# The low halves of every second weight block formed by GpSimd in place of VectorE, in a hybrid pooling and SSD decoder layer

## The chip, the cores and the metric

The kernel runs on one core of a Trainium2 chip. A core has TensorE for matrix products (PE in the profile; its weight loads are PEld), VectorE (DVE), ScalarE (ACT), GpSimd (POOL) and SyncE (SP), and queues through which SyncE, ScalarE and GpSimd issue DMA transfers. The engines run at the same time, each through its own list of instructions in a fixed order, and wait for one another by semaphores. The metric is device microseconds of one execution, lower being better.

## The reference

One decoder layer over 512 tokens and 16 leading meta tokens, width 1024, all in float32. Cut to what matters:

```python
h = concat([meta, x]); u = rmsnorm(h, mix_norm_w)
proj = u @ w_in[i]                     # 1024 x 9248: pooling input, z, xBC, dt, two gates
gates = sigmoid(gate columns + b_gate)
y_pool = pool_mixer(u_pool, ...) @ w_pool_up      # causal means over 2, 4, 8, 16 positions
y_ssd = mamba2_branch(z, xbc, dt, ...) @ w_ssd_out  # conv, SSD in chunks of 128, 8 groups
h = h + (gate_pool * y_pool + gate_ssd * y_ssd) @ w_o
v = rmsnorm(h, mlp_norm_w)
hid = relu(v @ w_ff1); h = h + (hid * hid) @ w_ff2
return rmsnorm(h, final_norm_w)[:, 16:]
```

## The kernel before

Activations are kept transposed, features on the 128 partitions and tokens along the free axis. Every float32 operand of a product is split into two float32r tiles: a high half, the cast of the operand, and a low half, the operand less its high half. A product is then three matmuls: high by high, high by low, low by high.

**Weight blocks.** The weights come as 128x1024 blocks in the order in which they are used. `block_tiles` (line 63) takes the next number from the counter `nblk` and three tiles: `raw` from a ring of 3, `whi` and `wlo` from rings of 4. `block_part` (line 70) then issues three instructions: SyncE's load of `raw` (line 72), ScalarE's cast to `whi` (line 73) and VectorE's subtraction to `wlo` (line 74). The tiles of a block can be written again when the block that had them before is through on TensorE, so up to three blocks are prepared ahead. The same counter is advanced by loads of weights that don't pass through `block_part` (`wo_load`, line 706, and `quarter`, line 904); those are split by `split` (line 713, ScalarE's cast and VectorE's subtraction in lines 717 and 718).

**Stages in time.**
- Until about 68 us: the input norm, the first group's projections on the not yet normalised input, three gates, `dt` and its sums (lines 175 to 326 and 520 to 526).
- The loop over eight groups (line 562), about 68 to 484 us. For each group `ssd` (line 383) is woven with `group_proj` (line 351) of the next group. `ssd` loads `abc` by GpSimd's DMA queue (line 391) and makes decay factors of it on ScalarE and VectorE; VectorE multiplies them by the masked product of C and B (line 457, 128x2048), and TensorE takes the result as an operand of `py` (line 470). A chain of chunk states `st` runs beside it, on VectorE, two steps for each chunk (lines 455 and 456): the first reads two tiles in SBUF, the second one in SBUF and one in PSUM. TensorE takes the states as operands of `po` (line 464). `group_proj` takes up four projections `px` and, by `conv` (line 328), has ScalarE and VectorE read them out of PSUM (lines 331 and 334), then two projections `pz`. With group 4, `out_half` (line 544) forms half of the SSD output projection; with the last, `out_part` (line 552) a further part, which VectorE adds onto `acc` (line 559).
- About 484 to 563 us: the pooling branch (`pool_tile`, line 580, with running sums `pw` on VectorE in lines 593 and 595; `pool_mix`, line 603) and the last part of the SSD output projection, `psl`, added onto `acc` (line 633).
- About 563 to 640 us: the SSD gates and the pooling branch's projection, merged (lines 729 to 744); then the output projection by a Strassen-like scheme of seven products (lines 748 to 864), to about 690 us.
- The MLP (from line 867). There GpSimd forms sums of weight quarters (`sum_of`, line 965, its instruction in line 967).

Which instruction stands where on an engine is decided by a scheduler when the kernel is built, by its own estimates of durations; it keeps the data dependences and puts in the semaphores. An engine then runs its list in that order, so an instruction that waits holds all behind it on its engine. Beside its set-up, GpSimd has this list before: the four stores of `acs_d` (line 302), the eight loads `abc` (line 391), four loads of `ht` and one of `fw` (lines 754 and 755), and the 28 sums of line 967.

Of the kernel before, what the change touches and what calls it, by code (L numbers as in the profile page):

```python
# [9 lines left out]
F32 = mybir.dt.float32  # L10
F32R = mybir.dt.float32r
AF = mybir.ActivationFunctionType
ALU = mybir.AluOpType
# [36 lines left out]
def kernel(ctx: ExitStack, tc, xT, x, w, vec, fnw, out):  # L50
    nc = tc.nc
    act, dve, pe, pool = nc.scalar, nc.vector, nc.tensor, nc.gpsimd
# [6 lines left out]


    nblk = [0]

    def block_tiles():
        b = nblk[0]
        nblk[0] += 1
        return (b, wp.tile([P, 1024], F32, tag="raw", name=f"raw{b}", bufs=3),
                wp.tile([P, 1024], F32R, tag="whi", name=f"whi{b}"),
                wp.tile([P, 1024], F32R, tag="wlo", name=f"wlo{b}"))

    def block_part(t, c):  # L70
        b, raw, hi, lo = t
        nc.sync.dma_start(raw[:, c], w[b, :, c])
        act.copy(hi[:, c], raw[:, c])  # L73
        dve.tensor_tensor(lo[:, c], raw[:, c], hi[:, c].bitcast(F32), op=ALU.subtract)  # L74

    def block():
        t = block_tiles()
        block_part(t, slice(0, 1024))
        return t[2:]
# [8 lines left out]
    def mm3(ps, a, b, first, last):  # L88
        (ah, al), (bh, bl) = a, b
        pe.matmul(ps, ah, bh, start=first, stop=False)  # L90
        pe.matmul(ps, ah, bl, start=False, stop=False)  # L91
        pe.matmul(ps, al, bh, start=False, stop=last)  # L92
# [88 lines left out]
    b, raw, hi, lo = wdt  # L181
# [18 lines left out]
    dve.tensor_tensor(spread(lo)[:, :2], once[:, :2], spread(hi)[:, :2].bitcast(F32), op=ALU.subtract)  # L200
    x_split(0)
    block_part(wB, slice(0, 256))
    x_load(1)
    proj_step(dt_runs, 0, wdt[2:], X)
# [3 lines left out]
    dve.tensor_tensor(spread(lo)[:, 2:], once[:, 2:], spread(hi)[:, 2:].bitcast(F32), op=ALU.subtract)  # L208
    x_load(2)
    block_part(wB, slice(256, 1024))  # L210
    proj_step(dt_runs, 1, wdt[2:], X)
    proj_step(runsB, 1, wB[2:], X)
# [45 lines left out]
    for i in range(2):  # L258
        pb = psum1(f"pb1_{i}")
        c = slice(3 * i, 3 * i + 3)  # L260
# [77 lines left out]
    def group_tiles(g):  # L338
        xc = gc.tile([P, 2, L], F32, tag="xc", name=f"xc{g}")
        bt = gc.tile([P, L], F32, tag="bt", name=f"bt{g}")  # L340
        ct = gc.tile([P, SEQ], F32, tag="ct", name=f"ct{g}")
        zt = gc.tile([P, 2, SEQ], F32, tag="zt", name=f"zt{g}", bufs=1)
        return xc, bt, ct, zt
# [7 lines left out]
    def group_proj(g, cur, gate=None):  # L351

        first = g == 0
        xc, bt, ct, zt = cur
        for dst, t, skip in ((bt, 16 + g, 0), (ct, 24 + g, NM - 4), (xc[:, 0, :], 2 * g, 0),
                             (xc[:, 1, :], 2 * g + 1, 0)):
            if first and dst is bt:
                view = viewB
            else:
                runs, view = wide(psum2(f"px{g}_{t}"), skip)  # L360
                proj(runs, block(), X if first else U)
            conv(dst, first_raw(t, view, skip) if first else view, t)
            yield
        if gate is not None:
            gate_pool(gate)
            yield
        ps = psum2(f"pz{g}")
        for i in range(2):
            proj(narrow(ps[:, i * SEQ : (i + 1) * SEQ]), block(), X if first else U)
        zf = zt.rearrange("p i t -> p (i t)")  # L370
        if first:
            dve.tensor_tensor(zt, ps.rearrange("p (i t) -> p i t", i=2),
                              rsb[:, NM:].unsqueeze(1).to_broadcast([P, 2, SEQ]), op=ALU.mult)
            act.activation(zf, zf, AF.Silu)
        else:
            act.activation(zf, ps, AF.Silu)
        yield
# [125 lines left out]
    def weave(a, b, n):  # L503

        end = object()
        a = [a]
        while a or b:
            for s in [a] + [b] * n:
                if s and next(s[0], end) is end:
                    s.pop(0)  # L510
# [33 lines left out]
    def out_half():  # L544
        for dd in range(4):
            ps = psum2(f"pso{dd}")
            for i in range(2):
                ssd_out(2 * dd + i, ps[:, i * SEQ : (i + 1) * SEQ], range(8))
                act.copy(acc[2 * dd + i], ps[:, i * SEQ : (i + 1) * SEQ])
                yield  # L550

    def out_part():

        un = units()
        for d in range(NK):
            ps = psum2(f"psp{d}")[:, :SEQ]
            for k in range(8, 14):
                mm3(ps, next(un), ys[k], k == 8, k == 13)
            dve.tensor_tensor(acc[d], acc[d], ps, op=ALU.add)
            yield  # L560

    for g in range(G):
        nxt = group_tiles(g + 1) if g + 1 < G else None
        fill = [group_proj(g + 1, nxt, GATE_AT.get(g))] if nxt else [out_part()]
        if g == 4:
            fill = [out_half()] + fill
        weave(ssd(g, cur), fill, 2 if g == 4 else 1)
        cur = nxt
# [160 lines left out]
    for n, d in enumerate(MERGE):  # L729
# [8 lines left out]
        for i, k in enumerate(ks):  # L738
            c = slice(k * P, (k + 1) * P)
# [131 lines left out]
    def ff1_part(p, ks, first, last):  # L871
        ps, wh, wl = p
        for k in ks:
            cs = slice(k * P, (k + 1) * P)
            mm3(ps, (wh[:, cs], wl[:, cs]), (vh[k], vl[k]), first and k == ks[0], last and k == ks[-1])
# [7 lines left out]
    ff1_part(pf[1], range(4, 8), True, False)  # L883
    for p in pf:
        ff1_part(p, range(4), False, True)
    wo2_stack.close()
    mg_stack.close()
    wo_stack.close()
# [145 lines left out]
    c = NC - 1  # L1034
# [172 lines left out]
```

## Time and profile before

| what | value |
|---|---|
| time, median of 2 runs (lowest, highest) | 1025.61 us (1025.49, 1025.72) |
| span of the profiled execution, first to last instruction | 1023.3 us |
| time of the profiled execution beside its span | not given; the median is 2.3 us above the span |
| TensorE busy | 1014.6 us (99%) |
| VectorE busy | 730.3 us (71%), 954 instructions |
| ScalarE busy | 552.5 us (54%) |
| GpSimd busy | 88.7 us (9%), 52 instructions |
| granted TensorE clock, mean | 0.999 |
| DMA | 105.63 MB, 103 GB/s over the span |

Times in the profile are microseconds from the span's start, unless marked ns. A row of the timeline gives start, duration, engine, line, operation, the tiles written and read with their shapes and, in brackets, how long the engine had been idle before it and what ended that. Equal instructions that follow each other are one row, with their count. A group row gives busy time in us and mean duration in ns, then idle time before the instructions and who ended it. A row of the waits says which engine and line waited for which, for how many us in total, how many times, and the longest. A row of stretches gives the stretch and its length, busy time (and instructions) of PE, PEld, DVE, ACT and POOL, the granted clock, the DMA share and GB/s. Matmuls are pipelined and their ends are modelled, so their durations overlap.

### The profile page before, as it was taken

The page shows a single profiled execution, that of the slowest core. Times are in us where ns is not written, and L with a number is a line of the kernel's source. Part 1 is how long each engine was busy: PE and PEld are TensorE (multiplying, and loading weights), DVE is VectorE, ACT ScalarE, POOL GpSimd, SP SyncE. Part 2 cuts the span into 40 slices and gives each one's busy share as a digit, 9 for nine tenths or more (in the row PEclk, how much of TensorE's full clock was granted, in tenths as well). Part 3 has the DMA queues.
Part 4 walks back from the last instruction along what each step waited for, and adds up shares of the span by engine and source line. Part 5 has one row for each costly group of instructions (what it writes and reads, how often), then busy time and mean ns, then how long its engine had stood idle before and what let it go on. Part 6 is the DMA issues. An engine that isn't in the chain of part 4 may idle for free.

```text
span 1023.3 us, 14063 instructions
## 1 busy us (share of the span) xinstructions
PE 1014.6 (99%) x5697; PEld 876.7 (86%) x5697; DVE 730.3 (71%) x954; ACT 552.5 (54%) x728; POOL 88.7 (9%) x52
## 2 busy tenths in 40 slices
PE   9999999999999999999999999999999999999997
PEld 8889989998879898988899888888888888888886
DVE  7978788687746586978755457975777577666866
ACT  7775968586627339573244343474545355454444
POOL 0100000000000000000000001003040421413400
PEclk9999999999999999999999999999999999999999
DMA  7243051414332331414532333224323323334112
GB/s 237 72 160 103 21 166 38 148 46 141 102 101 86 103 104 42 145 41 141 189 102 84 103 104 120 86 91 156 103 69 122 120 83 113 95 102 124 42 42 83
DMA packets 29281, 105.63 MB, mean 103 GB/s; under 512 B 3296, under 2 KB 4256, under 8 KB 28192
## 3 DMA queue, kind: packets, MB, share of 16 engines
q1 hardware_dynamic: 26496, 92.75, 28.7%
q0 software_dynamic: 2000, 11.08, 3.0%
q8 instruction: 45, 0.74, 0.3%
q10 hardware_dynamic: 720, 0.91, 0.3%
q14 instruction: 20, 0.16, 0.1%
HBM read 102.55 MB, written 2.16 MB: 102 GB/s over the span
## 4 chain that ended last, share of the span: by engine, by line
PE 96%; DVE 2%; ACT 0%; DMA 0%; issue 0%; SPq 0%; ACTq 0%
PE px L143 6%; PE px L144 6%; PE pf L92 6%; PE pf L91 6%; PE px L146 6%; PE pf L90 6%; PE alpha L956 3%; PE alpha L957 3%; PE alpha L958 3%; PE pz L143 3%; PE pz L146 3%; PE pz L144 3%; PE py L470 2%; PE pso L90 2%; PE pp L144 2%; PE pp L146 2%
## 5 line engine op out<-in xcount | busy, mean ns | idle before, releaser
L73 ACT CAST whi<-raw 128x1024 fp32r<-128x1024 f32 (+1 forms) x131 | 135.7, 1043 | 220.0 <-PE pf L91 55.8
L74 DVE TENSOR_TENSOR wlo<-raw,whi 128x1024 fp32r<-128x1024 f32 (+1 forms) x131 | 163.6, 1251 | 112.6 <-ACT whi L73 105.3
L143 PE MATMUL px<-uh,whi 128*128 128x264 f32 (+1 forms) x448 | 121.2, 290 | 0.7 <-DVE ct L334 0.7
L144 PE MATMUL px<-ul,whi 128*128 128x264 f32 (+1 forms) x448 | 118.9, 285 | 0.0
L90 PE MATMUL pf<-vh,whi 128*128 128x512 f32 x256 | 99.8, 390 | 0.0
L92 PE MATMUL pf<-vh,wlo 128*128 128x512 f32 x256 | 99.6, 389 | 0.0
L91 PE MATMUL pf<-vl,whi 128*128 128x512 f32 x256 | 99.6, 389 | 0.0
L146 PE MATMUL px<-uh,wlo 128*128 128x264 f32 (+1 forms) x448 | 90.8, 284 | 0.0
L143 PEld LDWEIGHTS px<-uh,whi 128*128 128x128 f32 x448 | 84.6, 189 | 2.8 <-issue 2.6
L144 PEld LDWEIGHTS px<-ul,whi 128*128 128x128 f32 x448 | 84.8, 189 | 0.3
L718 DVE TENSOR_TENSOR slo<-b,shi 128x1024 fp32r<-128x1024 f32 x35 | 49.1, 1403 | 31.6 <-ACT shi L717 31.6
L146 PEld LDWEIGHTS px<-uh,wlo 128*128 128x128 f32 x448 | 69.4, 188 | 0.3 <-issue 0.3
L717 ACT CAST shi<-b 128x1024 fp32r<-128x1024 f32 x35 | 36.8, 1050 | 47.2 <-PE pf L91 36.4
L91 PEld LDWEIGHTS pf<-vl,whi 128*128 128x128 f32 x256 | 48.1, 188 | 10.0
L90 PEld LDWEIGHTS pf<-vh,whi 128*128 128x128 f32 x256 | 48.1, 188 | 9.9
L92 PEld LDWEIGHTS pf<-vh,wlo 128*128 128x128 f32 x256 | 48.1, 188 | 9.9
L967 POOL TENSOR_TENSOR b<-b,b 128x1024 f32<-128x1024 f32 x14 | 35.7, 2548 | 238.3 <-DVE slo L718 238.3
L956 PE MATMUL alpha<-shi,hh 128*128 128x512 f32 x140 | 54.6, 390 | 0.0
L957 PE MATMUL alpha<-slo,hh 128*128 128x512 f32 x140 | 54.5, 389 | 0.0
L958 PE MATMUL alpha<-shi,hl 128*128 128x512 f32 x140 | 54.5, 389 | 0.0
L783 DVE TENSOR_TENSOR ht<-ht,alpha 128x1024 f32<-128x1024 f32 x35 | 42.5, 1214 | 10.9 <-PE alpha L958 10.9
L143 PE MATMUL pz<-uh,whi 128*128 128x512 f32 x112 | 44.0, 393 | 0.0
(412 smaller groups left out, 2513.7 us busy)
## 6 DMA issues: line engine op xcount, KB each, us to landing
raw<-in_w SPq DMA_DIRECT2D x129, 512.0 KB, 3.6
b<-in_w SPq DMA_DIRECT2D x28, 512.0 KB, 3.6
abc<-acs_d POOLq DMA_DIRECT2D x8, 1024.0 KB, 7.2
wob<-in_w SPq DMA_DIRECT2D x8, 512.0 KB, 4.6
xt<-in_xT SPq DMA_DIRECT2D x8, 264.0 KB, 5.6
ht<-in_x POOLq DMA_DIRECT2D x4, 512.0 KB, 6.7
w<-in_w SPq DMA_DIRECT2D x4, 512.0 KB, 3.6
out_dram<-out SPq DMA_DIRECT2D x4, 320.0 KB, 2.4
```

The lines of the kernel that those rows point to most:

```text
L73: act.copy(hi[:, c], raw[:, c])
L74: dve.tensor_tensor(lo[:, c], raw[:, c], hi[:, c].bitcast(F32), op=ALU.subtract)
L90: pe.matmul(ps, ah, bh, start=first, stop=False)
L91: pe.matmul(ps, ah, bl, start=False, stop=False)
L92: pe.matmul(ps, al, bh, start=False, stop=last)
L143: pe.matmul(o, wh, rhs[0][k][:, c], start=k == 0, stop=False)
L144: pe.matmul(o, wh, rhs[1][k][:, c], start=False, stop=False)
L146: pe.matmul(o, wl, rhs[0][k][:, c], start=False, stop=k == NK - 1)
L718: dve.tensor_tensor(lo, src, hi.bitcast(F32), op=ALU.subtract)
L956: pe.matmul(ps[t], a[0], wh[:, cs], start=f, stop=False, skip_group_check=True)
L957: pe.matmul(ps[t], a[0], wl[:, cs], start=False, stop=False, skip_group_check=True)
L958: pe.matmul(ps[t], a[1], wh[:, cs], start=False, stop=l, skip_group_check=True)
```

## The change

From the loop over the groups on, a flag is set, and while it is set `block_part` gives the subtraction of a block with an odd number to GpSimd and that of an even one to VectorE. The flag is taken back after the first two blocks of the MLP's first product have been prepared; from there on all are VectorE's again. Operands, shapes and the numbers computed stay the same. By the counter this concerns 45 blocks. The scheduler, which sees the other engine, also places some instructions of TensorE, VectorE, ScalarE and SyncE otherwise, mostly within the loop over the groups.

```diff
@@ -59,6 +59,7 @@
     nblk = [0]
+    by_pool = [False]
 
     def block_tiles():
         b = nblk[0]
@@ -71,7 +72,8 @@
         b, raw, hi, lo = t
         nc.sync.dma_start(raw[:, c], w[b, :, c])
         act.copy(hi[:, c], raw[:, c])
-        dve.tensor_tensor(lo[:, c], raw[:, c], hi[:, c].bitcast(F32), op=ALU.subtract)
+        on = pool if by_pool[0] and b % 2 else dve
+        on.tensor_tensor(lo[:, c], raw[:, c], hi[:, c].bitcast(F32), op=ALU.subtract)
@@ -559,6 +561,7 @@
+    by_pool[0] = True
     for g in range(G):
         nxt = group_tiles(g + 1) if g + 1 < G else None
@@ -883,6 +886,7 @@
     for p in pf:
         ff1_part(p, range(4), False, True)
+    by_pool[0] = False
     wo2_stack.close()
```

## The prediction

> **What bounds the kernel now.** I read the busy shares first, then the chain that ended last, then the list of what TensorE waited for, then the engines' busy time stage by stage.
>
> ```profile
> PE 1014.6 (99%) x5697; PEld 876.7 (86%) x5697; DVE 730.3 (71%) x954; ACT 552.5 (54%) x728; POOL 88.7 (9%) x52
> PE 96%; DVE 2%; ACT 0%; DMA 0%; issue 0%; SPq 0%; ACTq 0%
> ...
> PE pdt L187 <- DVE ones_r L100: 1.5, 1, 1.5
> PE px L143 <- DVE ct L334: 0.7, 1, 0.7
> PE pdt L143 <- ACT xh L194: 0.2, 1, 0.2
> PE pt_dt L305 <- DVE ddt L294: 0.2, 1, 0.2
> ...
> 68.00:264.00 196.00, 195.32 (x1370) 177.56 (x1369) 152.47 (x242) 141.29 (x189) 2.12 (x4) 1.00 0.29 90
> 442.00:484.00 42.00, 42.00 (x225) 34.66 (x223) 38.46 (x54) 21.86 (x31) 0.00 (x0) 1.00 0.29 88
> 484.00:563.00 79.00, 79.00 (x526) 72.59 (x526) 50.56 (x66) 29.99 (x40) 0.00 (x0) 1.00 0.39 127
> 563.00:640.00 77.00, 77.00 (x338) 63.14 (x337) 45.81 (x64) 26.23 (x34) 2.60 (x5) 1.00 0.36 110
> ```
>
> TensorE is busy 99% of the span and is 96% of the chain. All its waits of the whole run are those four rows, 2.6 us, and three of them lie before the stretch that the change touches (about 57 to 680 us). Columns of the stretches are length, then PE, PEld, DVE, ACT, POOL. From 68 to 264 us TensorE lacks 0.68 us (196.00 less 195.32), the one wait of line 143 for VectorE's `ct`; in the three later stretches it lacks nothing. So whatever VectorE is spared, **at most 0.7 us can be won**. What can be lost is open: VectorE is busy 78% (152.47 of 196) and 92% (38.46 of 42) of the first two stretches, so it does not run far ahead of TensorE there.
>
> **What is removed and added.** The block counter runs over all weight blocks, so the odd ones from 11 to 85, then 89, 91, 95, 97, 101, 103 and 107 go over: 45 subtractions. (The counter is also advanced by the blocks that bypass this path, so near the end two of three neighbours can be odd.) DMAs, casts and matmuls stay, as does their number.
>
> ```profile
> L74 DVE TENSOR_TENSOR wlo<-raw,whi 128x1024 fp32r<-128x1024 f32 x86 | 104.8, 1220 | 74.2 <-ACT whi L73 66.9 <-PE po L464 7.3
> ...
> 755.68 1.22 DVE L783 TENSOR_TENSOR ht<-ht,alpha 128x1024 f32<-128x1024 f32 x1 [0.64 <-PE alpha L958]
> 756.82 1.79 DVE L74 TENSOR_TENSOR wlo<-raw,whi 128x1024 fp32r<-128x1024 f32 x1
> 761.98 2.33 DVE L718 TENSOR_TENSOR slo<-t,shi 128x1024 fp32r<-128x1024 f32 x1 [3.37 <-ACT shi L717]
> 764.24 1.21 DVE L74 TENSOR_TENSOR wlo<-raw,whi 128x1024 fp32r<-128x1024 f32 x1
> ...
> 755.12 2.41 POOL L967 TENSOR_TENSOR b<-b,b 128x1024 f32<-128x1024 f32 x1 [33.09 <-DVE slo L718]
> 757.61 3.25 POOL L967 TENSOR_TENSOR t<-b,b 128x1024 f32<-128x1024 f32 x1
> 760.82 2.40 POOL L967 TENSOR_TENSOR b<-b,b 128x1024 f32<-128x1024 f32 x1
> 764.39 3.32 POOL L967 TENSOR_TENSOR t<-t,b 128x1024 f32<-128x1024 f32 x1 [1.16 <-DVE slo L718]
> ...
> 712.05 2.89 DVE L938 TENSOR_TENSOR s<-r 128x512 f32<-128x512 f32 x1
> ```
>
> VectorE loses 45 x 1.220 = 54.9 us. GpSimd gains 45 operations of the shape that its sums of line 967 have: 2.40 us when nothing is beside them, up to 3.32, so 45 x 2.40 = 108 to 45 x 3.32 = 149 us in a stretch of 620. It is far from full.
>
> **The hold between the two engines.** These rows, all of the last stage, also show what the pairing costs. VectorE's `ht<-ht,alpha` (one operand in PSUM) ran in the middle of GpSimd's 755.12 operation in its usual 1.22. `wlo` and `slo`, with both operands in SBUF, did not: `slo` came at 761.98, GpSimd's operation ended at 763.22, and `slo` took 2.33 for 1.22, that is 763.2 plus its own length. Turned round, `wlo` began at 764.24 and the GpSimd operation of 764.39 took 3.32 for 2.40. So whoever comes second stands still until the first has ended. The dearest hold here is `s<-r` at 712.05, a 128x512 form that takes 0.68 elsewhere (the `acc` row below has that size): 2.89, a hold of 2.2. One moved block thus spares VectorE 1.22 and costs it between 0 and 2.2. The saving and the hold are about equal in sum; they are not equal in place. VectorE's queue had the subtraction *behind* the urgent work, GpSimd does it as soon as the cast is ready.
>
> The Trainium skill ("SBUF — State Buffer", Who interferes with whom) says that a VectorE instruction with two SBUF inputs contends with a GpSimd one that reads SBUF, and that the second to issue is blocked fully, not slowed. The trace agrees by the 2.33 for 1.22 above; by that rule the worst hold is one whole GpSimd operation, 2.40 in place of 2.2, and 45 of them would take back 108 us of VectorE for 54.9 given.
>
> **Is the low half there in time?** Mostly sooner than before, since VectorE often got to it late. The nearest call is block 59:
>
> ```profile
> 403.62 1.98 ACT L73 CAST whi<-raw 128x1024 fp32r<-128x1024 f32 x2
> ...
> 408.74 0.40 PE L146 MATMUL px<-uh,wlo 128*128 128x258 f32 x2
> ```
>
> Block 59 is the first of the two casts, so ready at 404.7; TensorE wants the low half at 408.74. GpSimd needs 2.40 to 3.32: done at 407.1 to 408.0. It holds by 0.7 us; cost 0. If it were held twice, 1 to 2 us. Every other moved block has more room.
>
> **GpSimd's queue.** The eight loads `abc` (line 391) were alone on it; in the built order they now stand behind low halves, and a low half that waits for its cast keeps the load behind it waiting. The two closest:
>
> ```profile
> 138.81 0.53 POOL L391 DMA_DIRECT2D abc<-acs_d  x1 [44.98 <-PE py L470]
> 375.53 0.53 POOL L391 DMA_DIRECT2D abc<-acs_d  x1 [72.17 <-DVE wlo L74]
> abc<-acs_d POOLq DMA_DIRECT2D x8, 1024.0 KB, 7.2
> ...
> 135.42 1.06 ACT L73 CAST whi<-raw 128x1024 fp32r<-128x1024 f32 x1 [4.52 <-DMA raw<-in_w]
> 147.67 1.06 ACT L426 ACTIVATE eb<-abc 64x1024 f32<-64x1024 f32 x1
> ...
> 372.87 1.04 ACT L73 CAST whi<-raw 128x1024 fp32r<-128x1024 f32 x1 [2.38 <-PE px L144]
> 384.65 1.06 ACT L426 ACTIVATE eb<-abc 64x1024 f32<-64x1024 f32 x1
> ```
>
> The cast of 135.42 ends at 136.5, its low half on GpSimd at 138.9 to 139.8: the load goes out 0.1 to 1.0 us later than at 138.81, lands 7.2 later, at 146.1 to 147.0, and its reader is at 147.67. The other: cast done 373.9, low half 376.3 to 377.2, load landed by 384.4, read at 384.65. Both fit; cost 0. If they missed by a microsecond, ScalarE would be late by that, and the `abc` work has most of a stage before its product. The five loads of lines 754 and 755 go out after all but one of the moved operations. The other way round, a load that waits for its buffer holds the low halves behind it; of the casts that follow a load in that queue none was ready before its load's present issue. Cost 0.
>
> **Where a hold reaches TensorE.** Two places, one of each kind.
>
> ```profile
> 122.18 2.95 ACT L73 CAST whi<-raw 128x1024 fp32r<-128x1024 f32 x3
> ...
> 121.38 2.29 DVE L457 TENSOR_TENSOR abc<-abc,cbm 128x2048 f32<-128x2048 f32 x1 [0.19 <-ACT abc L436]
> 124.26 0.42 DVE L455 TENSOR_TENSOR st<-st,cdec 128x256 f32<-128x256 f32 x1
> 126.27 0.42 DVE L455 TENSOR_TENSOR st<-st,cdec 128x256 f32<-128x256 f32 x1
> ...
> 127.03 1.09 PE L470 MATMUL py<-abc,xdt 128*64 128x128 f32 x16
> 130.39 0.36 PE L143 MATMUL px<-uh,whi 128*128 128x264 f32 x1 [0.68 <-DVE ct L334]
> ...
> 496.32 1.05 ACT L73 CAST whi<-raw 128x1024 fp32r<-128x1024 f32 x1
> ...
> 497.78 0.69 DVE L593 TENSOR_TENSOR pw<-pw 128x525 f32<-128x525 f32 x1
> 498.40 1.22 DVE L74 TENSOR_TENSOR wlo<-raw,whi 128x1024 fp32r<-128x1024 f32 x1
> 500.15 0.68 DVE L633 TENSOR_TENSOR acc<-acc,psl 128x512 f32<-128x512 f32 x1
> ...
> 500.88 0.50 PE L90 MATMUL psl<-yh,whi 128*128 128x512 f32 x1
> ```
>
> *Group 1, 122 to 132 us.* The middle one of the three casts is block 19, moved; it ends at about 124.2, and GpSimd is at it until 126.6. The new order sets VectorE's large product `abc` (2.29) behind the second `st` step of this list, where it was ahead of the first. Without it ahead, the second step can come up to 2.2 sooner, at 124.1 at the earliest, and `abc` can end at 126.7, in time for `py` (127.03, and about 127.1 in the new order, one matmul later). But a step that falls after 124.2 is held to 126.6; it then ends at 126.9 and `abc` at 129.2: TensorE waits 129.2 - 127.1 = 2.1 us. The wait of 0.68 at 130.39 goes, as the new TensorE order has that block's matmuls later. Net +1.4.
>
> *The `psl` accumulations, 496 to 501 us.* Block 75's cast ends at 497.37; GpSimd has SBUF until 499.8. The `pw` step of 497.78 starts there and not at 497.78: +2.0, less the 1.22 of `wlo` that is gone from behind it. The `acc` addition comes at 500.4 for 500.15, and TensorE, which goes on at 500.88, 0.05 after that addition's end at 500.83, is late by 0.2 to 0.3. Net +0.3.
>
> The other six groups have the same `st` chain with a moved cast somewhere near it. I take 0 for them as the likeliest: no other wait of TensorE stands in the list, so they have margin, and the saved 1.22 comes to it. The dearest is group 1's 1.4 each, 6 x 1.4 = 8.4, and the cheapest 0, for nothing more can be won.
>
> **Sum**: +1.4 + 0.3 = +1.7 on a span of 1023.3. The page gives the profiled run no time beside its span; the median of the runs shown, 1025.61, is 2.3 above it, which I keep: 1025.6 + 1.7 = **1027.3**.
>
> **Rivals.**
> - *VectorE's relief wins.* The 54.9 us spared arrive ahead of the chains, no hold reaches TensorE, and the 0.68 wait goes: 1025.6 - 0.7 = 1024.9. For it: 74.2 us of idle before `wlo`, most of it for the cast, no longer stand at the head of VectorE's queue. Against it: the place of block 19.
> - *A hold in every group.* Up to 1.4 in each of seven, plus 0.3: 1025.6 + 10.1 = 1035.7. For it: the chain is alike in all groups. Against: margins differ.
> - *Slower beyond 2%.* The same hold, struck twice in each of seven groups' `st` chains: 2 x 2.1 less the 1.22 spared is 3.0, times 7 is 21, 1025.6 + 21 = 1046.6. It decides from 20.5 / 7 = 2.9 us of wait in each group. Against it: TensorE that waits lets VectorE catch up.
> - *GpSimd's queue makes low halves or `abc` late.* Block 59's 0.7 of room and the two loads' 0.2 and 0.7 are overrun by 1 to 2 us each: 1027.3 + 3 = 1030.3.
>
> That the change is not carried out can be left out: the built order shows all 45 on GpSimd.
>
> **Chances.** Forecast (1025.5 to 1029) 0.57; relief 0.16; queue late 0.08; a hold in every group 0.15; beyond 2% 0.04. Range 1024.5 to 1034: it takes in relief, forecast and queue (0.81) and the lower half of the hold in every group. Within 2% (20.5 us, about what a measurement of this kernel can tell from no change) lie all but the last: 0.95; slower 0.04; 0.01 for faster, which the 0.7 rules out unless the profile hides waits in busy time.
>
> **What would show it.** Line 74's subtraction (or the new line's) 45 times on POOL at 2.4 to 3.3; VectorE busy less by clearly less than 54.9; two-operand forms of 0.4 to 0.7 with some of 2 to 3 us; in the list of TensorE's waits new rows for `abc` or `py` near 127 us and for `acc` near 501, in all 1 to 3 us. It is wrong if TensorE waits for `wlo` on POOL, if its waits pass 10 us, or if the span falls by more than 1 us.

## The result, and the profile after

The changed kernel takes 1036.49 us (median of 2, 1035.62 to 1037.37) against 1025.61 before: ratio 1.0107, 95% interval 1.0077 to 1.0136. That is 10.9 us slower, within the 2% but outside the predicted range (1024.5 to 1034), and near the rival "a hold in every group" (1035.7).

The busy shares from the page of the changed kernel; then its list of TensorE's waits; then its stages, with the columns explained above; last two short stretches of group 2:

```profile
PE 1018.8 (98%) x5697; PEld 878.7 (85%) x5697; DVE 723.9 (70%) x909; ACT 552.5 (53%) x728; POOL 204.0 (20%) x97
...
PE po L466 <- DVE st L458: 6.2, 7, 1.7
PE pdt L189 <- DVE ones_r L102: 1.5, 1, 1.5
PE psl L92 <- DVE acc L636: 1.5, 1, 1.5
PE py L472 <- issue: 0.6, 1, 0.6
...
68.00:264.00 196.00, 191.05 (x1331) 173.29 (x1330) 145.22 (x215) 133.23 (x175) 35.25 (x17) 0.99 0.28 91
264.00:350.00 86.00, 86.00 (x502) 74.08 (x501) 48.31 (x68) 46.83 (x69) 18.34 (x8) 1.00 0.33 105
350.00:442.00 92.00, 90.07 (x651) 82.30 (x650) 63.35 (x91) 49.70 (x65) 18.53 (x9) 1.00 0.29 92
442.00:484.00 42.00, 41.61 (x220) 33.39 (x219) 33.51 (x51) 27.49 (x36) 7.21 (x4) 1.00 0.24 75
484.00:563.00 79.00, 77.42 (x505) 70.38 (x504) 49.75 (x61) 26.79 (x35) 19.15 (x8) 1.00 0.38 127
...
180.00:184.00 4.00, 3.76 (x25) 3.31 (x26) 2.29 (x5) 1.48 (x2) 0.00 (x0) 0.65 0.42 136
184.00:188.00 4.00, 4.00 (x32) 4.00 (x32) 3.96 (x6) 0.64 (x1) 0.00 (x0) 0.92 0.02 4
```

Three things are to be seen. VectorE was relieved of 45 subtractions, 54.9 us by the durations of their rows, and its busy time fell by only 6.4 (730.3 to 723.9). And TensorE, which lacked 0.68 us in these stages, now lacks 4.95, 0, 1.93, 0.39 and 1.58, together 8.85. The waits that are new are those for the state `st` (seven times, 6.2 us), for the addition `acc` (1.5) and two ahead of `py` (0.6 and 0.3). No row names GpSimd: TensorE never waits for a low half.

The third is that waits are not the whole loss. The span grew by 11.9 us (1023.3 to 1035.2), and 4.2 of them are busy time of TensorE (1014.6 to 1018.8), for the same 5697 matmuls. By the last two rows the granted clock fell to 0.65 and 0.92 in group 2, directly behind two waits of 1.16 and 1.15 us; in the kernel before it is 1.00 in both stretches. That is worth some 1.7 us, an estimate (0.35 and 0.08 of 4 us each). Where the other 2.5 us lie was not taken apart.

Where the states became late is in one group row. Of the 24 state steps with both operands in SBUF, first the kernel before, then the changed one (count, busy time, mean ns of one):

```profile
L455 DVE TENSOR_TENSOR st<-st,cdec 128x256 f32<-128x256 f32 x24 | 10.0, 417 | 0.3 <-ACT st L453 0.2
```

```profile
L457 DVE TENSOR_TENSOR st<-st,cdec 128x256 f32<-128x256 f32 x24 | 22.0, 918 | 0.3 <-ACT st L455 0.2
```

The same 24 instructions take 12.0 us more. Group 3 in the changed kernel's timeline (start, duration) shows how:

```profile
224.73 2.28 DVE L459 TENSOR_TENSOR abc<-abc,cbm 128x2048 f32<-128x2048 f32 x1
226.93 0.76 DVE L336 SCALAR_TENSOR_TENSOR bt<-px,vs,bt 128x525 f32<-128x525 f32 x1
227.61 1.96 DVE L457 TENSOR_TENSOR st<-st,cdec 128x256 f32<-128x256 f32 x1
234.20 2.53 DVE L457 TENSOR_TENSOR st<-st,cdec 128x256 f32<-128x256 f32 x1
...
224.71 4.58 POOL L76 TENSOR_TENSOR wlo<-raw,whi 128x1024 fp32r<-128x1024 f32 x1 [1.26 <-ACT whi L74]
234.07 2.38 POOL L76 TENSOR_TENSOR wlo<-raw,whi 128x1024 fp32r<-128x1024 f32 x1 [4.79 <-ACT whi L74]
...
237.78 0.49 PE L466 MATMUL po<-ct,st 128*128 128x128 f32 x2 [1.68 <-DVE st L458]
```

GpSimd's subtraction of 224.71, which the profile begins 0.02 before VectorE's `abc`, nevertheless stands behind it for 2.2 us (4.58 for 2.38). When `abc` ends, it is GpSimd's turn, and the state step of 227.61 stands until 229.3 (1.96 for 0.42). VectorE's `bt` between the two, with one operand in PSUM, ran in its usual 0.76. At 234.07 GpSimd is first by 0.13 us, the last state step takes 2.53, and TensorE stands 1.68 us. Group 6 repeats both holds (417.43 with 1.96, 423.89 with 2.59).

### The profile page after: what moved, and what is told of

It is laid out like the page before. It is cut to its first block, busy times and chain, and to the rows that moved or that the text cites. A ratio compares the mean times of both kernels' runs of the same rounds, so it can differ in the third digit from the quotient of the medians.

```text
span 1035.2 us, 14097 instructions
## 1 busy us (share of the span) xinstructions
PE 1018.8 (98%) x5697; PEld 878.7 (85%) x5697; DVE 723.9 (70%) x909; ACT 552.5 (53%) x728; POOL 204.0 (20%) x97
## 4 chain that ended last, share of the span: by engine, by line
PE 84%; DVE 7%; ACT 5%; issue 3%; DMA 1%; POOL 0%; ACTq 0%; DVEq 0%; POOLq 0%
PE pf L94 6%; PE pf L93 6%; PE pf L92 6%; PE px L145 5%; PE px L146 4%; PE px L148 4%; PE alpha L960 3%; PE alpha L962 3%; PE alpha L961 3%; PE pz L148 2%; PE pz L145 2%; PE pz L146 2%; PE py L472 2%; PE pso L92 2%; PE pso L94 1%
## 5 line engine op out<-in xcount | busy, mean ns | idle before, releaser
L76 POOL TENSOR_TENSOR wlo<-raw,whi 128x1024 fp32r<-128x1024 f32 x45 | 115.2, 2559 | 482.6 <-ACT whi L74 458.7
L76 DVE TENSOR_TENSOR wlo<-raw,whi 128x1024 fp32r<-128x1024 f32 (+1 forms) x86 | 109.5, 1275 | 87.0 <-ACT whi L74 84.5
L786 DVE TENSOR_TENSOR ht<-ht,alpha 128x1024 f32<-128x1024 f32 x35 | 42.6, 1217 | 10.9 <-PE alpha L962 10.9
```

Of the source, the lines that this page charges most:

```text
L76: on.tensor_tensor(lo[:, c], raw[:, c], hi[:, c].bitcast(F32), op=ALU.subtract)
```

## Experiments

The change does two things at once: GpSimd and VectorE can now hold one another, and the scheduler issues other instructions in another order (in groups 2 and 4 `abc` now comes ahead of the first state step, in groups 1, 5 and 7 later than before). **Hold** is the theory that the first costs the time, **order** that the second does. In most of the kernels below the lists of TensorE, VectorE, ScalarE and SyncE are fixed, instruction by instruction, to those of the kernel before ("old order") or of the changed kernel ("new order"), by dependences that set the order of issue and add no wait; GpSimd's own list and the 45 subtractions are left to the scheduler. All ratios are against the kernel before on the same chip, which took 1025.0 to 1025.2 us there.

### GpSimd subtracts, old order

```diff
-        on.tensor_tensor(lo[:, c], raw[:, c], hi[:, c].bitcast(F32), op=ALU.subtract)
+        ins = on.tensor_tensor(lo[:, c], raw[:, c], hi[:, c].bitcast(F32), op=ALU.subtract)
+        if on is pool:
+            moved.add(ins.ins.name)
...
     assert nblk[0] == w.shape[0], (nblk[0], w.shape)
+    _hold_order(tc, nc, moved)
```

> GpSimd forms the 45 low halves as in the changed kernel, but TensorE, VectorE, ScalarE and SyncE issue everything else in the order in which the kernel before issues it. Two theories of the 10.9 us that the change lost. Hold: a VectorE product that meets a GpSimd subtraction stands still until that ends, and where this product is one of the steps to the state TensorE waits; the order matters little, so the time stays at 1033 to 1037 us and VectorE's busy time near the 723.9 us of the changed kernel. Order: the new order puts the 2.28 us product abc ahead of a state step, which makes the state late without any hold; with the old order back the time falls to 1025 to 1027 us.

Measured: 1031.07 us (1030.85 to 1031.26), ratio 1.0059 (1.0044 to 1.0074). It lies between the two expectations: 5.4 us of the loss go with the new order, and about 6 stay with the old.

### The subtractions left out, new order and old order

```diff
-        on = pool if by_pool[0] and b % 2 else dve
-        on.tensor_tensor(lo[:, c], raw[:, c], hi[:, c].bitcast(F32), op=ALU.subtract)
+        if by_pool[0] and b % 2:
+            return
+        dve.tensor_tensor(lo[:, c], raw[:, c], hi[:, c].bitcast(F32), op=ALU.subtract)
...
         block_part(t, slice(0, 1024))
+        if by_pool[0] and t[0] % 2:
+            return t[2], t[2]
```

> The 45 subtractions are left out, on GpSimd and on VectorE; in these blocks TensorE reads the high half where it read the low half, so its work is the same in size and the part of the output that the low halves give is wrong. Everything else is issued in the order of the changed kernel. Hold: nothing is there to hold, so 1025 to 1026 us and a VectorE busy time of about 730.3 less 54.9, 675 us. Order: the late state steps remain, 1033 to 1037 us.

> The 45 subtractions are left out as in the kernel beside it, and everything else is issued in the order of the kernel before. Both theories: 1024.9 to 1025.6 us. It tells what VectorE's relief of 54.9 us is worth at most, when nothing is paid for it: the wait of 0.68 us of the prediction, or nothing.

Measured: new order 1023.63 us (1023.16 to 1024.27), ratio 0.9987 (0.9977 to 0.9996); old order 1025.29 (1025.10 to 1025.59), ratio 1.0003 (0.9994 to 1.0012). The page of the first, and its state steps:

```profile
PE 1013.6 (99%) x5697; PEld 876.3 (86%) x5697; DVE 681.5 (67%) x909; ACT 551.4 (54%) x728; POOL 88.6 (9%) x52
L478 DVE TENSOR_TENSOR st<-st,cdec 128x256 f32<-128x256 f32 x24 | 10.0, 417 | 0.1
```

The order theory falls: with nothing on GpSimd the new order is no loss but 1.7 us better than the old one, and 1.4 under the least that the hold theory expected. In the new order GpSimd's subtractions cost 12.9 us (1036.49 less 1023.63; 12.3 if each is taken against the kernel before that was measured beside it), in the old order 5.8 (1031.07 less 1025.29). So the holds cost the time, and the order decides how many of them fall on a step that TensorE waits for. VectorE's busy time says what it was held for in the new order: 723.9 less 681.5, 42.4 us. It also says what the relief is: 730.3 less 681.5, 48.8 us and not 54.9, since the rows of neighbouring VectorE instructions overlap by some 0.1 us. And the relief in itself is worth nothing in the old order: 45 subtractions fewer, and 1025.29 us for 1025.0.

### GpSimd writes and hardly reads, new order

```diff
+        e = slice(c.start, c.start + 1)
+        ins = [pool.tensor_tensor(lo[:, e], raw[:, e], hi[:, e].bitcast(F32), op=ALU.subtract)]
+        for _ in range(2):
+            ins.append(pool.memset(lo[:, c.start + 1 : c.stop].bitcast(F32), 0.0))
...
```

> In the 45 blocks GpSimd subtracts one column and then writes zeros over the other 1023 columns twice, so that it is busy for a like time at the same place, but reads next to nothing (the part of the output that these low halves give is left out). Order of the changed kernel. If GpSimd's reading is what holds VectorE: no holds, VectorE busy near 681 us, time 1023.4 to 1025 us. If any GpSimd instruction of that length holds it, or if GpSimd's queue and the later low halves cost the time: 1031 to 1036 us.

Measured: 1023.51 us (1023.21 to 1024.11), ratio 0.9984 (0.9974 to 0.9993), the same as with nothing on GpSimd. Group rows of this kernel:

```profile
L481 DVE TENSOR_TENSOR st<-st,cdec 128x256 f32<-128x256 f32 x24 | 10.1, 420 | 0.3 <-ACT st L479 0.2
L99 POOL MEMSET wlo<- 128x1023 f32 x90 | 85.8, 953 | 343.4 <-PE px L172 83.8 <-PE wo_q L799 38.7 <-PE pgp L172 38.5
```

GpSimd is busy 2 us in each of the same 45 places (1.9 in two writes, 0.25 in the one column), with the low half ready about as late as after a subtraction that isn't held (2.4 us), and no state step is held. GpSimd's queue and the time at which it delivers are thereby out. What goes with the hold is that GpSimd reads SBUF; a GpSimd instruction of another kind that reads as much was not tried. The Trainium skill ("SBUF — State Buffer", Who interferes with whom) says the same: a VectorE instruction with two SBUF inputs contends with a GpSimd one that reads SBUF, not with one that only writes it. The run agrees, 10.1 us for these steps against 22.0.

### Twelve of the 45, and the other 33, new order

In the changed kernel's trace twelve GpSimd subtractions overlap a lengthened state step, a lengthened `abc` or the lengthened `pw` of the `psl` stage. One kernel leaves these twelve out, the other leaves out all but them.

```diff
-        on = pool if by_pool[0] and b % 2 else dve
+        if by_pool[0] and b % 2 and b in MEET:        # the other kernel: b not in MEET
+            return
+        on = pool if by_pool[0] and b % 2 else dve
...
```

> Order of the changed kernel; GpSimd forms 33 of the 45 low halves, and the twelve whose subtraction met the state chain of a group, the product abc ahead of it or the window sum pw (blocks 19, 25, 27, 33, 35, 39, 41, 55, 61, 63, 67, 75) are left out, with TensorE reading the high half there. Place: only a hold on the steps that TensorE waits for costs time, so this falls nearly to the 1023.6 us of the order without any subtraction, 1023.5 to 1026 us, though VectorE is still held by the other 33. Sum: if VectorE's held time as such costs, then 33 of 45 of the 12.9 us stay, about 1033 us.

> The complement: GpSimd forms the low halves of those twelve blocks alone, the other 33 are left out. Place: nearly all the loss is here, 1032 to 1036 us. Sum: 12 of 45 of the 12.9 us, about 1027 us.

Measured: without the twelve 1025.70 us (1025.27 to 1026.14), ratio 1.0007 (0.9997 to 1.0016); with the twelve alone 1032.70 (1028.71 to 1033.31), ratio 1.0063 (1.0041 to 1.0085). The page and the state steps, first without the twelve, then the twelve alone with its waits:

```profile
PE 1015.1 (99%) x5697; PEld 876.6 (86%) x5697; DVE 706.9 (69%) x909; ACT 551.2 (54%) x728; POOL 168.7 (16%) x85
L483 DVE TENSOR_TENSOR st<-st,cdec 128x256 f32<-128x256 f32 x24 | 10.1, 420 | 0.3 <-ACT st L481 0.2
```

```profile
PE 1016.0 (99%) x5697; PEld 876.6 (85%) x5697; DVE 700.2 (68%) x909; ACT 551.7 (54%) x728; POOL 123.9 (12%) x64
L483 DVE TENSOR_TENSOR st<-st,cdec 128x256 f32<-128x256 f32 x24 | 22.0, 916 | 0.2
...
PE po L492 <- DVE st L484: 4.9, 5, 1.7
...
PE psl L118 <- DVE acc L662: 1.5, 1, 1.5
```

This is the place theory. Thirty-three subtractions hold VectorE for 25.4 us (706.9 less 681.5) and cost 2.1 us of time; twelve hold it for 18.7 us (700.2 less 681.5) and cost 9.1, by waits for `st` and `acc` as in the changed kernel. In the profile of the twelve the granted clock is 1.00 in every stretch of 4 us from 60 to 1020 us, so these 9.1 are not the clock's. The two sum to 11.2 of the 12.9.

### The meeting blocks back on VectorE, old order

```diff
-        on = pool if by_pool[0] and b % 2 else dve
+        on = pool if by_pool[0] and b % 2 and b not in MEET else dve
```

> Order of the kernel before. The ten odd blocks whose GpSimd subtraction met the state chain or abc in that order (19, 25, 27, 31, 33, 39, 41, 61, 67, 75) go back to VectorE at their old places, GpSimd forms the other 35. Place: the loss of 5.8 us in this order goes, 1025 to 1026 us, equal to the kernel before; nothing is to be gained, since without any of the 45 subtractions this order took 1025.3 us. Sum: 35 of 45 of 5.8 us stay, 1029.5 us.

Measured: 1025.74 us (1025.42 to 1026.13), ratio 1.0006 (0.9997 to 1.0015). Thirty-five blocks can go to GpSimd without a loss that this measurement tells from none (0.7 us), if these ten don't. Nothing is won either.

### Shorter holds: each subtraction in four

```diff
+        for k in range(4):
+            q = slice(c.start + 256 * k, c.start + 256 * k + 256)
+            pool.tensor_tensor(lo[:, q], raw[:, q], hi[:, q].bitcast(F32), op=ALU.subtract)
```

> As the first kernel (GpSimd subtracts, the order of before), but each GpSimd subtraction is cut into four of 256 columns, some 0.6 us each. Hold: if a VectorE product waits for the one GpSimd instruction that is running, no hold is longer than about 0.6 us, and the time falls to 1026 to 1029 us; if GpSimd's next quarter goes ahead of the waiting product, the holds are as long as before and the time is as in the first kernel. Order: no change against the first kernel, 1025 to 1027 us in both.

> Each GpSimd subtraction cut into four of 256 columns, in the order of the changed kernel. Hold: the holds stay under 1 us as in the quarters with the order of before, so most of the 12.9 us by which the changed kernel stands above the same order without subtractions (1036.5 against 1023.6) goes: 1024 to 1027 us. If instead it is the sum of the holds that counts, not their length, half of it stays (VectorE lost 23 us to holds with quarters and 40 us with whole subtractions in the order of before): about 1030 us.

> The changed kernel with each GpSimd subtraction cut into four of 256 columns, and no order imposed: the plain edit that a reader could make. Hold: 1024 to 1028 us, by the order that the scheduler then finds. It is the candidate to be as fast as the kernel before or faster.

Measured: old order 1026.63 us (1026.18 to 1027.87), ratio 1.0017 (1.0007 to 1.0026); new order 1029.77 (1027.98 to 1030.13), ratio 1.0039 (1.0024 to 1.0053); free order 1029.18 (1028.53 to 1031.14), ratio 1.0039 (1.0024 to 1.0054). So cutting the operation takes 4.4 of 5.8 us back in the old order, as expected of a hold by the one instruction that is running. In the new order it misses the expectation by 3 us, in the free order by 1.2. The 1029.77 is what the other theory there, the sum of the holds, expected (about 1030), but the kernels of twelve and 33 blocks speak against that one: 25.4 us of holds cost 2.1. The state steps in the new order, GpSimd's eight pieces for two blocks in group 4, and ScalarE and VectorE behind them:

```profile
L480 DVE TENSOR_TENSOR st<-st,cdec 128x256 f32<-128x256 f32 x24 | 13.9, 579 | 0.3 <-ACT st L478 0.2
...
267.80 8.63 POOL L98 TENSOR_TENSOR wlo<-raw,whi 128x256 fp32r<-128x256 f32 x8 [20.36 <-ACT whi L92]
...
277.32 1.05 ACT L92 CAST whi<-raw 128x1024 fp32r<-128x1024 f32 x1 [5.45 <-DMA raw<-in_w]
...
278.41 1.23 DVE L94 TENSOR_TENSOR wlo<-raw,whi 128x1024 fp32r<-128x1024 f32 x1 [6.03 <-ACT whi L92]
279.55 0.42 DVE L480 TENSOR_TENSOR st<-st,cdec 128x256 f32<-128x256 f32 x1
```

Here the states are late without being held. GpSimd, itself held by `abc`, takes 8.63 us for two blocks; the next load of `raw` lands late; ScalarE's cast waits 5.45 us for it; and VectorE's own subtraction, which the new order has *ahead* of the state steps, waits 6.03 with the states behind it. With the subtractions left out, in the same order, that cast waited only for TensorE and came 4.6 us sooner:

```profile
272.67 1.04 ACT L92 CAST whi<-raw 128x1024 fp32r<-128x1024 f32 x1 [1.37 <-PE pso L114]
```

That the ring of three `raw` tiles is the link is read from these rows; a fourth `raw` tile, which would test it, wasn't tried. TensorE waits 1.4 us for the states of this group, of 2.6 in the whole run, and there too the granted clock falls behind the waits, to 0.90 from 280 to 284 us and 0.67 from 284 to 288: another 1.7 us, an estimate as above.

### VectorE subtracts, new order

```diff
-        on = pool if by_pool[0] and b % 2 else dve
-        on.tensor_tensor(lo[:, c], raw[:, c], hi[:, c].bitcast(F32), op=ALU.subtract)
+        ins = dve.tensor_tensor(lo[:, c], raw[:, c], hi[:, c].bitcast(F32), op=ALU.subtract)
+        if by_pool[0] and b % 2:
+            moved.add(ins.ins.name)
```

> VectorE forms all low halves again, as in the kernel before; everything else is issued in the order of the changed kernel. Tells the new order from the relief: the order with the 45 subtractions left out took 1023.6 us, 1.4 less than before. If the order alone does that, 1023.5 to 1024.2 us here; if VectorE's relief is needed for it, 1025 us or more, since the 54.9 us of subtractions stand ahead of the state steps again.

Measured: 1032.56 us (1030.18 to 1033.68), ratio 1.0073 (1.0056 to 1.0090). The new order is good only if VectorE doesn't form these 45 low halves in it. How much of this is the order's is open: the places of the 45 subtractions in VectorE's list were the scheduler's own here, and three subtractions stand between the state steps of group 2, where the changed kernel has one:

```profile
176.20 2.36 DVE L93 TENSOR_TENSOR wlo<-raw,whi 128x1024 fp32r<-128x1024 f32 x2
178.47 0.42 DVE L476 TENSOR_TENSOR st<-st,cdec 128x256 f32<-128x256 f32 x1
178.80 1.22 DVE L93 TENSOR_TENSOR wlo<-raw,whi 128x1024 fp32r<-128x1024 f32 x1
179.94 0.42 DVE L477 TENSOR_TENSOR st<-st,pst 128x256 f32<-128x256 f32 x1
...
180.41 0.49 PE L485 MATMUL po<-ct,st 128*128 128x128 f32 x2 [2.39 <-DVE st L477]
```

No version that computes everything was faster than the kernel before.

## Why the prediction was wrong

**What bounds the kernel, and at most 0.7 us to win: near.** The kernels without the subtractions show what there was to win: nothing in the old order, 1.4 us (1025.0 to 1023.63) in the new one. The bound counted only the wait that the trace showed and missed that another order could gain a little more.

**Removed and added: right.** 45 on GpSimd, 2.4 us each when alone; in the changed kernel's page:

```profile
L76 POOL TENSOR_TENSOR wlo<-raw,whi 128x1024 fp32r<-128x1024 f32 x45 | 115.2, 2559 | 482.6 <-ACT whi L74 458.7
```

115.2 us, inside the 108 to 149.

**The hold between the two engines: right in kind.** "Whoever comes second stands still", 0 to 2.2 us, is what the rows of group 3 show from both sides, and the largest state step is 2.59 for 0.42. The saving and the hold were called about equal in sum; in busy time the holds took 42.4 us of the 48.8 spared. The 54.9 added up row durations that overlap.

**Is the low half there in time, and GpSimd's queue: right.** TensorE has no wait for a low half, and with GpSimd only writing, at the same places of the same queue, the time is 1023.5 us. Cost 0, as said.

**Group 1, net +1.4: too dear.** The changed kernel's rows there:

```profile
122.77 2.42 POOL L76 TENSOR_TENSOR wlo<-raw,whi 128x1024 fp32r<-128x1024 f32 x1 [20.61 <-ACT whi L74]
...
123.57 1.90 DVE L457 TENSOR_TENSOR st<-st,cdec 128x256 f32<-128x256 f32 x1
125.39 2.28 DVE L459 TENSOR_TENSOR abc<-abc,cbm 128x2048 f32<-128x2048 f32 x1
...
127.77 0.62 PE L472 MATMUL py<-abc,xdt 128*64 128x128 f32 x6 [0.64 <-issue]
```

The mechanism is the one described: the second state step is held, `abc` behind it ends at 127.67, `py` starts 0.10 later. But GpSimd's subtraction came at 122.77 and not at 124.2, so `abc` ended 1.5 us sooner than the 129.2 I had, and TensorE stood 0.64, not 2.1. The wait of 0.68 for `ct` went, as predicted. The net is about 0.

**The `psl` accumulations, +0.3: too cheap.** First two rows of the kernel before, then the changed one:

```profile
499.24 0.39 PE L92 MATMUL psl<-yh,wlo 128*128 128x512 f32 x1
499.47 0.40 PE L90 MATMUL pg<-ph,whi 128*128 128x512 f32 x1
```

```profile
507.60 2.40 POOL L76 TENSOR_TENSOR wlo<-raw,whi 128x1024 fp32r<-128x1024 f32 x1 [10.37 <-ACT whi L74]
...
507.93 2.63 DVE L596 TENSOR_TENSOR pw<-pw 128x525 f32<-128x525 f32 x1
510.48 0.68 DVE L636 TENSOR_TENSOR acc<-acc,psl 128x512 f32<-128x512 f32 x1
...
509.36 0.40 PE L94 MATMUL psl<-yh,wlo 128*128 128x512 f32 x1
511.21 0.50 PE L92 MATMUL psl<-yh,whi 128*128 128x512 f32 x1 [1.46 <-DVE acc L636]
```

The hold of `pw` is 1.94, the 2.0 predicted, and the 1.22 credited against it came too: `acc` starts 2.55 us after `pw`, where it was 2.37 (500.15 less 497.78). `pw` starts where it did in TensorE's work, 1.43 us ahead of the last `psl` matmul of the block before (509.36), for 1.46 ahead of 499.24. What failed is TensorE's side. In the kernel before six `pg` matmuls, from 499.47 to 500.88, stood between that matmul and the one that needs `acc`; in the new order the latter follows at once, so TensorE is there 1.4 us sooner. The prediction reckoned with TensorE's new order in group 1 and not here. In the old order, with the `pg` matmuls in place, the first kernel of the experiments waits 0.8 us for `acc`.

**The step that failed: "The other six groups ... I take 0 for them as the likeliest."** This is the term of the sum that was mis-sized. The reason given was that no other wait of TensorE stood in the list, "so they have margin". The list tells that the states were in time, not by how much. Asked by stretch, TensorE's waits for the states in the changed kernel are these, of groups 2 (170 to 200 us), 3 (225 to 250) and 6 (415 to 440):

```profile
PE po L466 <- DVE st L458: 2.3, 2, 1.2
...
PE po L466 <- DVE st L458: 2.0, 3, 1.7
...
PE po L466 <- DVE st L458: 1.9, 2, 1.7
```

They sum to the 6.2 of the whole run. In each of these three groups two instructions of one chain are held: two state steps in groups 3 and 6, in group 2 `abc` (3.20 for 2.29) and then a step (2.33 for 0.42). Where this order holds only one, group 1's step of 1.90 or group 4's `abc` of 4.17, TensorE waits for no state. So the bound of 1.4 in each, taken from group 1, was no bound. The rival "a hold in every group" came near the total by luck, with the wrong spread: three groups pay some 2 us each, four pay nothing for their states, and `psl` pays 1.5 and not 0.3. The rival "slower beyond 2%" described a hold struck twice, but in all seven groups and at 3.0 us each.

A second term stood at nothing without a reason: the sum added waits alone to the span, as if TensorE's work itself would take no longer. It took 4.2 us longer, some 1.7 of it at the lower clock behind group 2's waits.

**The scheduler's new order** entered the prediction only at group 1. By the runs it is why the loss is 10.9 and not about 6. Two of its effects could have been read from the built order: the six `pg` matmuls that no longer stand ahead of `psl`, and `abc` put ahead of group 2's state steps.

## What to carry to other kernels

Moving work from VectorE to GpSimd is not paid by the sum of busy time but by which VectorE instructions it meets: here 12 of 45 blocks made most of the loss, and 33 others that held VectorE for 25 us cost two. Before moving such work, list the VectorE instructions with two SBUF operands that TensorE waits for, find how long before its need each of them ends, and take any room under one whole GpSimd instruction as lost; no wait in the profile doesn't mean that there is room. If it must move, move the blocks that meet no such chain, or cut the GpSimd instruction into pieces shorter than the room; here the pieces took longer together than the whole (180 of 0.93 us in the mean, 3.7 a block, for 2.56 in the new order).

## What the runs showed of the hardware

- Two engines that hold each other took turns, in groups 3 and 6. GpSimd, let in behind `abc`, then held the next state step, so one GpSimd subtraction cost both engines some 2 us (4.58 for 2.38, 1.96 for 0.42).
- GpSimd's writes don't hold VectorE: 90 writes of 128x1023, 953 ns each, left the state steps at 10.1 us.
- A VectorE instruction with a single tensor operand in SBUF (and one scalar for each partition) can be held too. In the changed kernel, beside GpSimd's subtraction of 316.56 (to 318.95), a pair of `abc<-abc,dtok`, of which four take 0.86 elsewhere in the same kernel, took 1.77:

```profile
104.10 0.86 DVE L436 TENSOR_SCALAR abc<-abc,dtok 128x128 f32<-128x128 f32 x4
317.46 1.77 DVE L436 TENSOR_SCALAR abc<-abc,dtok 128x128 f32<-128x128 f32 x2 [1.82 <-ACT eb L428]
...
316.56 2.39 POOL L76 TENSOR_TENSOR wlo<-raw,whi 128x1024 fp32r<-128x1024 f32 x1 [6.50 <-ACT whi L74]
```

The Trainium skill ("SBUF — State Buffer", Who interferes with whom) lists `tensor_scalar` among the operations that can take the shared ports; the trace agrees with this one row. The prediction looked for two-operand forms alone.
- The same engines' lists in another order, with 45 subtractions left out in both, differ by 1.7 us (1023.63 and 1025.29).
- The granted clock fell behind TensorE's waits in some places and not in others: to 0.65 in the changed kernel's group 2 (waits of 1.16 and 1.15 us), to 0.67 with the quarters in group 4 (waits of 0.24, 0.50 and 0.65), but not behind the single wait of 1.68 us in the changed kernel's group 3. What decides it is not shown.
